# Attention units taken in pairs: scores and V products of neighbouring pairs in one break of the projection stream, transposes in another, and a new layout of PSUM

## The chip, the core and the metric

The kernel runs on one core of one Trainium2 chip. The time is the device time of one execution, in microseconds, and the figure for a kernel is the median of its runs. Engines are called by their names in the profile: PE (TensorE, with PEld for its weight loads), DVE (VectorE), ACT (ScalarE), POOL (GpSimd) and SP (SyncE, which issues most of the DMAs). "L187" is line 187 of the kernel.

## What is computed

One decoder layer over 256 tokens of width 1024, in fp32. The hidden state is normalised and projected once; two attention mixers read the projections; their results are merged through gates; then a feed-forward layer and a last normalisation follow. Cut to what matters here:

```python
h = rmsnorm(x, norm1_g[layer]);  proj = h @ w_in[layer]
# mixer A ("n"): 8 heads in 2 groups; compressed, selected and window branches
y_nsa  = gate0 * softmax(q kc) vc + gate1 * softmax(q_r ks) vs + gate2 * softmax(q_r kw) vw
# mixer B ("m"): 8 heads, causal attention with their own k and v
y_moba = softmax(qm km) vm
mixed = sig(gm[:, :1024]) * (y_nsa @ w_up_nsa) + sig(gm[:, 1024:]) * (y_moba @ w_up_moba)
x = x + mixed @ w_out
x = x + relu(rmsnorm(x, norm2_g) @ w_ff1) ** 2 @ w_ff2
return rmsnorm(x, norm_f_g)
```

With 256 tokens, all four selected blocks of 64 are always taken, and the window of 512 and the block of 256 cover everything, so the selected, window and block branches are plain causal attention.

## The kernel before

**The stream of chunks.** All weights are cut into 60 chunks of up to 128 x 2048 numbers (`CHUNKS`, L20). Each chunk is loaded by one DMA into `raw`, and split into two parts for the matmuls: `whi` by ACT (L87) and `wlo` by DVE (L89, `raw - whi`). A product is then three matmuls: high by high, high by low, low by high (`mm3`). There are three buffers of each; the split for chunk c+2 is made while PE works on chunk c, in two halves. The activations (`hTh`, `hTl` and so on) are split in the same way.

**Slots and events.** The time that PE spends on one chunk is a slot. The program calls `at(pos, f, ...)` to put an event at a position from 0 to 1 of the coming slot, and `run_slot` then issues the slot's matmuls in order and calls each event when its position is reached; events of one position keep the order in which they were put. The schedule is manual: each engine gets its instructions in exactly this order and takes them in this order. The usual events of a slot are the two halves of `whi` at 0.0 and 0.45 and the two halves of `wlo` at 0.3 and 0.46 (`std_events`). A projection slot (chunks 0 to 11) has 24 matmuls of 384 to 512 columns, a slot of the merge gates (chunks 12 to 19, "gm") has 48 of 256 columns.

**Attention between the projections.** Attention is cut into 12 units (`UNITS`): for each pair of heads p of mixer A one unit with the selected keys (b = 1) and one with the window keys (b = 2), and for mixer B one unit per pair of heads. Unit u runs in slots u+8 and u+9:

- `u_scores` (0.02): scores of two heads into the PSUM tile `S`, one bank per head, as 64-row matmuls two at a time; the first 128 queries go in exact fp32, the others by three matmuls of split parts.
- `u_max` (0.03, DVE): mask, row maxima, times -0.125.
- `u_exp` (0.34, ACT): four exponentials with row sums into `P`.
- `u_norm` (0.38, DVE): sums to factors, with the branch's gate for mixer A, and `P` times factor.
- `u_trans` (0.25 of the next slot): three transposes per head on PE into two `tp` banks; ACT copies one to `PT`, DVE the other.
- `u_pv` (0.8): products with V as 64-column matmuls into the bank `yb`; ahead of them, once per p of mixer A, the compressed branch (`bdv` by `pcT`, 30 rows). `u_yevac` (0.9): split into `yTh` (ACT) and `yTl` (DVE).

Around these stand, in the same slots, the rotary embedding (`rope`, DVE) and the transposes of the heads (`transp_heads`) of the next section, the compressed branch's probabilities (`cmp_scores`, `cmp_probs_t`), the evacuation of each section (`evac_tm`, ACT), and in the gm slots `gm_evac` of the slot before (0.5: DVE multiplication L568, then ACT tanh L570).

**PSUM.** Eight banks: three `acc` in turn, one `yb`, two `tp`, two for `S`. In the feed-forward stage `tp` and `S` give way to four banks `o`.

Of the kernel before, what the change touches and what calls it, by code (L numbers as in the profile page):

```python
# [8 lines left out]
F32 = mybir.dt.float32  # L9
F32R = mybir.dt.float32r  # L10
AF = mybir.ActivationFunctionType
ALU = mybir.AluOpType
# [28 lines left out]
def hybrid_layer(ctx: ExitStack, tc: tile.TileContext, gxd, w, w1c, small, const, gf, out):  # L41
# [6 lines left out]
    ps_acc = ctx.enter_context(tc.tile_pool(name="ps_acc", bufs=3, space=PS))  # L48
    ps_y = ctx.enter_context(tc.tile_pool(name="ps_y", bufs=1, space=PS))
    at_stack = ExitStack()  # L50
    ap_ = at_stack.enter_context(tc.tile_pool(name="att", bufs=1))
    ps_t = at_stack.enter_context(tc.tile_pool(name="ps_t", bufs=2, space=PS))
    ps_s = at_stack.enter_context(tc.tile_pool(name="ps_s", bufs=1, space=PS))
    ctx.enter_context(tc.manual_schedule())

    def acc_tile():
        return ps_acc.tile([128, 512], F32, name="acc")

    def tp_tile():
        return ps_t.tile([128, 512], F32, name="tp")  # L60
# [39 lines left out]
    warm = ps_y.tile([128, 512], F32, name="yb")  # L100
# [4 lines left out]
    kc_ = cp.tile([128, K_N], F32, name="kc")  # L105
    w1 = ap_.tile([128, 2, 16, 64], F32, name="w1", tag="w1")
# [192 lines left out]
    bdv = ap_.tile([128, 128], F32, name="bdv")  # L299
# [4 lines left out]

    def cmp_gather(s):
        tp = ps_y.tile([128, 512], F32, name="yb") if s else ps_s.tile([128, 2, 512], F32,
                                                                       name="S")[:, 0]
# [48 lines left out]
    pcT = ap_.tile([32, 4, 256], F32, name="pcT")  # L356
# [38 lines left out]
    UNITS = [("n", p, b) for p in range(4) for b in (1, 2)] + [("m", p, 0) for p in range(4)]  # L395

    def u_scores(u):
        kind, p, b = UNITS[u]
        qs = qrT if kind == "n" else qmT
        kk, kp = (ksT if b == 1 else kwT, 0) if kind == "n" else (kmT, p)  # L400
        S = ps_s.tile([128, 2, 512], F32, name="S")
# [504 lines left out]
```

## Time and profile before

| | us |
|---|---|
| median of 3 runs | 395.99 |
| lowest, highest | 395.7, 398.17 |
| the profiled execution's own time | 396.34 |
| its span, first to last instruction | 394.5 |
| PE busy in the span | 384.6 (97%) |
| DVE busy | 267.5 (68%) |
| ACT busy | 204.6 (52%) |
| POOL busy | 9.0 (2%) |
| from 59 to 163 us, the slots with attention units: PE, DVE, ACT busy of 104.0 | 104.0, 86.8, 62.0 |
| mean granted clock of PE | 0.99 |

The profile is of one execution. A timeline gives for each instruction, or run of like ones, its start and its length in microseconds, the engine, the line, the operation, the output and inputs with their shapes, and in brackets how long the engine stood idle before it and whose work ended that. Neighbouring instructions of one engine overlap, so the distance between two starts says what an instruction costs the queue. The ends of matmuls are modelled. A table of windows gives busy time of PE, PEld, DVE, ACT and POOL in a stretch, with counts, then the granted clock of PE as a share of full speed, and the DMA engines' share and rate.

### The profile page before, as it was taken

How to read it: one execution, taken by the hardware profiler on the slowest of the kernel's cores; microseconds unless marked ns; L12 is line 12 of the kernel's file. 1: busy time of each engine (PE TensorE's matmuls, PEld its weight loads, DVE VectorE, ACT ScalarE, POOL GpSimd, SP SyncE). 2: the span in 40 equal slices, each digit the busy share in tenths (PEclk: the TensorE clock that was granted, in tenths of full speed). 3: DMA queues.
4: the chain of work that ended last, by engine and by line, in shares of the span. 5: the costliest groups of instructions: out<-in, count | busy, mean ns of one | idle time of the engine just before them, and what ended most of it. 6: DMA issues, size and time to landing. Idle time of an engine off the chain costs nothing.

```text
span 394.5 us, 6611 instructions
## 1 busy us (share of the span) xinstructions
PE 384.6 (97%) x2687; PEld 346.3 (88%) x2687; DVE 267.5 (68%) x468; ACT 204.6 (52%) x366; POOL 9.0 (2%) x16
## 2 busy tenths in 40 slices
PE   7999999999999999999999999999999999999993
PEld 5888887778988999999999999999998888888883
DVE  5988589798778788867866665666566443444444
ACT  6474546667645555644464556455655563334412
POOL 4300000000000000000000000000000000000001
PEclk8799999999999999999999999999999999999999
DMA  7885623523323343263482655455544637555003
GB/s 240 313 339 214 213 106 114 207 89 126 108 108 107 124 157 149 108 214 106 171 311 96 226 214 185 154 197 213 185 154 195 213 130 268 169 184 208 1 2 106
DMA packets 11694, 66.34 MB, mean 168 GB/s; under 512 B 1296, under 2 KB 3600, under 8 KB 4368
## 3 DMA queue, kind: packets, MB, share of 16 engines
q1 hardware_dynamic: 11232, 65.14, 45.8%
q10 hardware_dynamic: 432, 0.79, 0.5%
q8 instruction: 21, 0.34, 0.3%
q14 instruction: 9, 0.07, 0.1%
HBM read 64.87 MB, written 1.05 MB: 167 GB/s over the span
## 4 chain that ended last, share of the span: by engine, by line
PE 93%; issue 2%; DMA 1%; DVE 1%; ACT 1%; SPq 0%; POOL 0%; POOLq 0%; DVEq 0%
PE acc L187 62%; PE o L187 21%; PE yb L187 3%; PE S L187 2%; PE tp L450 2%; PE tp L187 1%; DMA gx<-in_gx_dram 1%; PE tp L263 1%; DVE wlo L89 0%; PE acc L719 0%; POOL rstd L164 0%; PE tp L387 0%; SPq L71 0%; SPq L114 0%; DVE x L772 0%
## 5 line engine op out<-in xcount | busy, mean ns | idle before, releaser
L89 DVE TENSOR_TENSOR wlo<-raw,whi 128x1024 fp32r<-128x1024 f32 (+2 forms) x128 | 144.4, 1159 | 41.6 <-ACT whi L87 41.5
L87 ACT ACTIVATE whi<-raw 128x1024 fp32r<-128x1024 f32 (+2 forms) x128 | 124.1, 990 | 92.2 <-issue 35.5
L187 PE MATMUL acc<-h2h,whi 128*128 128x256 f32 x256 | 71.9, 281 | 0.0
L187 PE MATMUL acc<-h2l,whi 128*128 128x256 f32 x256 | 71.9, 281 | 0.0
L187 PE MATMUL acc<-h2h,wlo 128*128 128x256 f32 x256 | 71.9, 281 | 0.0
L187 PE MATMUL o<-whi,sqh 128*128 128x512 f32 (+1 forms) x128 | 49.5, 386 | 0.0
L187 PE MATMUL o<-whi,sql 128*128 128x512 f32 (+1 forms) x128 | 49.4, 386 | 0.0
L187 PE MATMUL o<-wlo,sqh 128*128 128x512 f32 (+1 forms) x128 | 49.4, 386 | 0.0
L187 PEld LDWEIGHTS acc<-h2h,whi 128*128 128x128 f32 x256 | 49.2, 192 | 0.0
L187 PEld LDWEIGHTS acc<-h2l,whi 128*128 128x128 f32 x256 | 48.0, 188 | 0.0
L187 PEld LDWEIGHTS acc<-h2h,wlo 128*128 128x128 f32 x256 | 48.0, 188 | 0.0
L187 PE MATMUL acc<-wlo,hTh 128*128 128x512 f32 (+2 forms) x96 | 38.7, 403 | 2.0 <-DVE wlo L89 1.8
L187 PE MATMUL acc<-whi,hTh 128*128 128x512 f32 (+2 forms) x96 | 38.1, 397 | 0.1
L187 PE MATMUL acc<-whi,hTl 128*128 128x512 f32 (+2 forms) x96 | 37.8, 394 | 0.0
L187 PE MATMUL acc<-hTh,whi 128*128 128x256 f32 x128 | 37.6, 293 | 0.0
L187 PE MATMUL acc<-hTl,whi 128*128 128x256 f32 x128 | 36.9, 289 | 0.0
L187 PE MATMUL acc<-hTh,wlo 128*128 128x256 f32 x128 | 36.2, 282 | 0.0
L187 PEld LDWEIGHTS o<-wlo,sqh 128*128 128x128 f32 x128 | 24.0, 188 | 4.9
L187 PEld LDWEIGHTS o<-whi,sql 128*128 128x128 f32 x128 | 24.0, 188 | 4.9
L187 PEld LDWEIGHTS o<-whi,sqh 128*128 128x128 f32 x128 | 24.0, 188 | 4.7
L187 PEld LDWEIGHTS acc<-hTh,whi 128*128 128x128 f32 x128 | 24.3, 190 | 1.4 <-issue 1.4
L187 PEld LDWEIGHTS acc<-hTl,whi 128*128 128x128 f32 x128 | 24.3, 190 | 1.0
(216 smaller groups left out, 613.5 us busy)
## 6 DMA issues: line engine op xcount, KB each, us to landing
raw<-in_ff_dram SPq DMA_DIRECT2D x32, 1024.0 KB, 4.8
raw<-in_gm_dram SPq DMA_DIRECT2D x8, 1024.0 KB, 4.8
raw<-in_wout_dram SPq DMA_DIRECT2D x4, 1024.0 KB, 4.9
raw<-in_q_dram SPq DMA_DIRECT2D x2, 1024.0 KB, 5.6
raw<-in_qm_dram SPq DMA_DIRECT2D x2, 1024.0 KB, 5.3
raw<-in_km_dram SPq DMA_DIRECT2D x2, 1024.0 KB, 4.9
raw<-in_vm_dram SPq DMA_DIRECT2D x2, 1024.0 KB, 4.8
raw<-in_upn_dram SPq DMA_DIRECT2D x2, 1024.0 KB, 4.7
```

What stands on the lines that cost most here:

```text
L87: act.activation(hi[c][:, a:b], raw[c][:, a:b], AF.Copy)
L89: dve.tensor_tensor(lo[c][:, a:b], raw[c][:, a:b], hi[c][:, a:b].bitcast(F32), op=ALU.subtract)
L187: pe.matmul(o, l, r, start=start, stop=stop, skip_group_check=True)
L263: pe.transpose(tp[:, j * 256 + t * 128:j * 256 + t * 128 + 128], src[:, t, (2 * i + j) * 128:(2 * i + j + 1) * 128], ident)
L450: pe.transpose(tp[:, dst:dst + 128], P[:, j, src:src + 128], ident)
```

## The change

Units are taken in pairs (`PAIRS`): the two branches of one p of mixer A, or two pairs of heads of mixer B. Pair d has slots 8 + 2d (even) and 9 + 2d (odd):

- even slot, 0.02: `d_scores` of pair d (four banks of `S`; the exact matmuls of both units at the end), and right behind it `d_pv` of pair d-1; 0.04 `d_yevac` of pair d-1; 0.05 `d_max`; 0.31 and 0.44 `d_exp` of the first and the second unit; 0.7 `d_norm`.
- odd slot, 0.5: `d_trans`: twelve transposes back into the banks of `S`, two copies of twice the width (ACT the first unit, DVE the second), and for mixer A the compressed branch's product, now over all 128 rows of `bdv` and `pcT`, which are zeroed at the start by POOL.

The softmax's DVE instructions work on both units at once: two masks and two row maxima of twice the width, and two multiplications of `P` by broadcast factors in place of eight by a scalar. `P` and `PT` have one buffer of twice the size in place of two.

PSUM: `S` has four banks, `acc` two (three from the second gm slot on, with `tp`), `tp` and `yb` one each. Until slot 9 `tp` and `yb` take turns for transposes. The first `S` also takes both transposes of `cmp_gather` and the accumulators of section "kvb"; the last one takes the four `o` banks of the second feed-forward product. The transposes of heads in slots 9 and 11 go from 0.5 and 0.65 to 0.3 and 0.75.

Of the diff, the core (lines that go away with `u_max` to `unit_events` are in the listing above and left out here):

```diff
...
+    ps = ctx.enter_context(tc.tile_pool(name="ps", bufs=1, space=PS))
...
+    turn = {"acc": ["acc0", "acc1"], "tp": ["tp", "yb"]}
+    def next_bank(kind):
+        t = turn[kind]
+        t.append(t.pop(0))
+        return bank(t[-1], kind)
     def acc_tile():
-        return ps_acc.tile([128, 512], F32, name="acc")
+        return next_bank("acc")
     def tp_tile():
-        return ps_t.tile([128, 512], F32, name="tp")
+        return next_bank("tp")
+    def s_tile():
+        return ps.tile([128, 4, 512], F32, name="S", tag="S")
...
+    pcT = ap_.tile([128, 4, 256], F32, name="pcT")
+    bdv = ap_.tile([128, 128], F32, name="bdv")
+    pool.memset(pcT, 0.0)
+    pool.memset(bdv, 0.0)
...
+    PAIRS = [[("n", p, 1), ("n", p, 2)] for p in range(4)] + [
+        [("m", p, 0), ("m", p + 1, 0)] for p in (0, 2)]
+    def d_scores(d):
+        S = s_tile()
         rows = [slice(j * 64, (j + 1) * 64) for j in range(2)]
-        for x, (a, b_) in enumerate(((1, 1), (1, 2), (2, 1))):
-            for j, r in enumerate(rows):
-                mm(S[:, j, 128:384], qs[a][r, p, :], kk[b_][r, kp, :], x == 0, x == 2)
-        for j, r in enumerate(rows):
-            mm(S[:, j, 0:128], qs[0][r, p, :], kk[0][r, kp, :], True, True)
-        d = {"S": S, "P": ap_.tile([128, 2, 384], F32, name="P", bufs=2),
-             "st": ap_.tile([128, 4, 4], F32, name="ust", bufs=2)}
-        U[u] = d
-
-    def u_max(u):
-        S, st = U[u]["S"], U[u]["st"]
-        for j in range(2):
-            v = S[:, j, :].rearrange("p (a b) -> p a b", a=4)[:, 0:3:2, :]
-            dve.tensor_tensor(v, v, cmask[:, None, :].to_broadcast([128, 2, 128]), op=ALU.add)
-        dve.tensor_reduce(st[:, 0, 0:2], S[:, :, 0:128], op=ALU.max, axis=AX)
-        dve.tensor_reduce(st[:, 0, 2:4], S[:, :, 128:384], op=ALU.max, axis=AX)
+        late = []
+        for x, (kind, p, b) in enumerate(PAIRS[d]):
+            qs = qrT if kind == "n" else qmT
+            kk, kp = (ksT if b == 1 else kwT, 0) if kind == "n" else (kmT, p)
+            for i, (a, b_) in enumerate(((1, 1), (1, 2), (2, 1))):
+                for j, r in enumerate(rows):
+                    mm(S[:, 2 * x + j, 128:384], qs[a][r, p, :], kk[b_][r, kp, :], i == 0, i == 2)
+            late += [(S[:, 2 * x + j, 0:128], qs[0][r, p, :], kk[0][r, kp, :])
+                     for j, r in enumerate(rows)]
+        for o, l, r in late:
+            mm(o, l, r, True, True)
+        U[d] = {"S": S, "P": ap_.tile([128, 4, 384], F32, name="P"),
+                "st": ap_.tile([128, 4, 8], F32, name="ust", bufs=2)}
+    def d_max(d):
+        S, st = U[d]["S"], U[d]["st"]
+        v = S.rearrange("p x (a b) -> p x a b", a=4)[:, :, 0:3:2, :]
+        for x in range(2):
+            w = v[:, 2 * x:2 * x + 2]
+            dve.tensor_tensor(w, w, cmask[:, None, None, :].to_broadcast([128, 2, 2, 128]),
+                              op=ALU.add)
+        dve.tensor_reduce(st[:, 0, 0:4], S[:, :, 0:128], op=ALU.max, axis=AX)
+        dve.tensor_reduce(st[:, 0, 4:8], S[:, :, 128:384], op=ALU.max, axis=AX)
         dve.tensor_scalar(st[:, 1], st[:, 0], -0.125, None, op0=ALU.mult)
+    def d_exp(d, x):
+        S, st, P = U[d]["S"], U[d]["st"], U[d]["P"]
         for t, a, b in ((0, 0, 128), (1, 128, 384)):
+            for j in (2 * x, 2 * x + 1):
+                i = t * 4 + j
                 act.activation(P[:, j, a:b], S[:, j, a:b], AF.Exp, scale=0.125,
                                bias=st[:, 1, i:i + 1], accum_out=st[:, 2, i:i + 1])
+    def d_norm(d):
+        st, P = U[d]["st"], U[d]["P"]
         dve.tensor_scalar(st[:, 2], st[:, 2], 1.0e-30, None, op0=ALU.max)
         dve.reciprocal(st[:, 3], st[:, 2])
+        kind, p, _ = PAIRS[d][0]
         if kind == "n":
+            v = st[:, 3].rearrange("p (t x h) -> p x t h", t=2, x=2)
+            for x in range(2):
+                dve.tensor_tensor(v[:, x], v[:, x], gates[:, 1 + x, p], op=ALU.mult)
+        for t, a, c in ((0, 0, 128), (1, 128, 384)):
+            v = P[:, :, a:c]
+            dve.tensor_tensor(v, v, st[:, 3, 4 * t:4 * t + 4, None].to_broadcast([128, 4, c - a]),
                               op=ALU.mult)
+    def d_trans(d):
+        S, P = U[d]["S"], U[d]["P"]
+        kind, p, _ = PAIRS[d][0]
+        PT = ap_.tile([128, 4, 384], F32, name="PT")
+        U[d]["PT"] = PT
+        for x in range(2):
+            for j in (2 * x, 2 * x + 1):
+                for c in (0, 128, 256):
+                    pe.transpose(S[:, j, c:c + 128], P[:, j, c:c + 128], ident)
+            v = slice(2 * x, 2 * x + 2)
+            if x == 0:
+                act.activation(PT[:, v], S[:, v, 0:384], AF.Copy)
             else:
+                dve.tensor_copy(PT[:, v], S[:, v, 0:384])
+        if d == 0:
+            U["y"] = bank("yb", "yb").rearrange("p (a q) -> p a q", a=2)
+        if kind == "n":
+            mm(U["y"][:, p % 2], bdv, pcT[:, p, :], True, False)
+    def d_pv(d):
+        PT = U[d]["PT"]
+        for x, (kind, p, b) in enumerate(PAIRS[d]):
+            y = U["y"][:, p % 2]
+            for t, n0 in ((0, 0), (1, 128)):
+                for j in range(2):
+                    if kind == "n":
+                        v = kvb[:, t, b * 128 + j * 64:b * 128 + (j + 1) * 64]
+                    else:
+                        v = vm[:, t, (2 * p + j) * 64:(2 * p + j + 1) * 64]
+                    rhs = PT[:, 2 * x + j, 0:256] if t == 0 else PT[:, 2 * x + j, 256:384]
+                    mm(y[j * 64:(j + 1) * 64, n0:256], v, rhs, kind == "m" and t == 0,
+                       t == 1 and (kind == "m" or b == 2))
+    def d_yevac(d):
+        kind, p, _ = PAIRS[d][0]
+        n = 1 if kind == "n" else 2
+        y = U["y"][:, p % 2:p % 2 + n]
+        h, l = yTh[kind][:, p:p + n, :], yTl[kind][:, p:p + n, :]
+        act.activation(h, y, AF.Copy)
+        dve.tensor_tensor(l, y, h.bitcast(F32), op=ALU.subtract)
+    def unit_events(s):
+        d, odd = (s - 8) // 2, s % 2
+        if not 8 <= s <= 20:
             return
+        if odd:
+            at(0.5, d_trans, d)
+            return
+        if d < 6:
+            at(0.02, d_scores, d)
+        if d > 0:
+            at(0.02, d_pv, d - 1)
+            at(0.04, d_yevac, d - 1)
+        if d < 6:
+            at(0.05, d_max, d)
+            at(0.31, d_exp, d, 0)
+            at(0.44, d_exp, d, 1)
+            at(0.7, d_norm, d)
...
-        accs = [acc_tile(), acc_tile()]
+        accs = [S_first[:, 2], S_first[:, 3]] if sec == "kvb" else [acc_tile(), acc_tile()]
...
-                at(0.5, transp_heads, tm["qm"], qmT, 0)
-                at(0.65, transp_heads, tm["qm"], qmT, 1)
+                turn["tp"] = ["tp"]
+                at(0.3, transp_heads, tm["qm"], qmT, 0)
+                at(0.75, transp_heads, tm["qm"], qmT, 1)
...
-                at(0.5, transp_heads, tm["km"], kmT, 0, False)
-                at(0.65, transp_heads, tm["km"], kmT, 1, False)
+                at(0.3, transp_heads, tm["km"], kmT, 0, False)
+                at(0.75, transp_heads, tm["km"], kmT, 1, False)
...
+        if i == 1:
+            turn["acc"].append("tp")
...
-    ops = {p: FB["o"].tile([128, 512], F32, name=f"o{p[0]}_{p[1]}") for p in PARTS[0] + PARTS[1]}
+    So = s_tile()
+    ops = {p: So[:, i] for i, p in enumerate(PARTS[0] + PARTS[1])}
...
```

More of the change, by code (lines that the diff above doesn't have):

```diff
@@ L713, in x1_rows @@
     def x1_rows():
-        tiles = [acc_tile(), acc_tile(), acc_tile(), ps_y.tile([128, 512], F32, name="yb")]
+        tiles = [acc_tile(), acc_tile(), acc_tile(), bank("yb", "yb")]
         for k2 in range(4):
@@ L812, in hybrid_layer @@
         else:
-            ops[LAST[1]] = ps_y.tile([128, 512], F32, name="yb")
+            ops[LAST[1]] = bank("yb", "yb")
             at(0.05, first_part)
```

80 lines of the change are left out of this document (5 added, 75 removed).

## The prediction

> **What bounds the kernel now.** I read the page first: span, and the chain of work that ended last.
>
> ```profile
> span 394.5 us, 6611 instructions
> ```
>
> ```profile
> PE 93%; issue 2%; DMA 1%; DVE 1%; ACT 1%; SPq 0%; POOL 0%; POOLq 0%; DVEq 0%
> ```
>
> The chain that sets the end is TensorE's own instruction stream for 93% of the span. So a change in the attention stage has two prices: what it does to the length of that stream, and any wait that it puts into it. For both I read the timeline of that stage, engine by engine. First TensorE around one unit's scores (columns: start, duration, engine, line, operation, tiles, count):
>
> ```profile
> 102.27 0.28 PE L187 MATMUL acc<-hTh,wlo 128*128 128x256 f32 x1
> 102.39 0.28 PE L187 MATMUL acc<-hTh,whi 128*128 128x256 f32 x1
> 102.60 0.39 PE L187 MATMUL S<-kwh,qrh 64*128 64x256 f32 x2
> 102.82 0.28 PE L187 MATMUL S<-kwl,qrh 64*128 64x256 f32 x2
> 102.94 0.28 PE L187 MATMUL S<-kwh,qrl 64*128 64x256 f32 x2
> 103.06 0.39 PE L187 MATMUL S<-kw,qr 64*128 64x128 f32 x4
> 103.37 0.38 PE L187 MATMUL acc<-hTl,whi 128*128 128x256 f32 x1
> 103.59 0.28 PE L187 MATMUL acc<-hTh,wlo 128*128 128x256 f32 x1
> ```
>
> Starts tell more than durations, because neighbours overlap. The projection's matmuls start 0.12 us apart (102.27, 102.39). Around the change to 64-row matmuls the steps are 0.21 or 0.22 instead (102.39 to 102.60, 102.60 to 102.82, 103.37 to 103.59), about 0.1 more each time. From 102.39 to 103.59 are 1.20 us where two steps of the stream would take 0.24: this break costs 0.96. Then a transposition, and the V products with the compressed branch ahead of them:
>
> ```profile
> 104.79 0.82 PE L450 MATMUL tp<-ident,P 128*128 128x128 f32 x6
> 105.36 0.36 PE L187 MATMUL acc<-hTh,whi 128*128 128x256 f32 x1
> 105.56 0.28 PE L187 MATMUL acc<-hTl,whi 128*128 128x256 f32 x1
> ...
> 108.55 0.28 PE L187 MATMUL acc<-hTh,wlo 128*128 128x256 f32 x1
> 108.76 0.69 PE L187 MATMUL yb<-pcT,bdv 30*128 30x256 f32 x2
> 109.38 0.87 PE L187 MATMUL yb<-PT,kvb 128*64 128x256 f32 x8
> 110.18 0.39 PE L187 MATMUL acc<-hTh,whi 128*128 128x256 f32 x1
> 110.40 0.28 PE L187 MATMUL acc<-hTl,whi 128*128 128x256 f32 x1
> ```
>
> Six transposes take 0.57 and 0.08 of delay behind them (0.20 for 0.12): 0.65. The V products cost 0.21 + 0.80 + 0.22 - 0.24 = 0.99, the compressed branch before them 0.62 (108.76 to 109.38).
>
> **Part 1, TensorE's stream.** A pair of units costs now 2 x 0.96 + 2 x 0.99 + 2 x 0.65 = 5.20, and 5.82 with the compressed branch (the four "n" pairs). Afterwards:
> - The joint break has 0.98 (102.39 to 103.37) for one unit's scores, 0.57 for the other's (three more steps of 0.12, and 0.21 for the second pair of exact matmuls: the 0.31 from 103.06 to 103.37 without 0.1 for the change of shape), 0.70 and 0.80 for two units' V products (the first saves the 0.1 of leaving), 0.22, less 0.24: 3.03.
> - The transposing break has 12 transposes: 0.65 + 0.57 = 1.22, and in "n" pairs the compressed branch, now over all 128 rows: 0.62 less the two changes of shape, 0.42.
>
> So 4.67 instead of 5.82 in four pairs and 4.25 instead of 5.20 in two: 6.5 us less. Pair 0's scores and pair 5's V products stand in breaks of their own, which gives back about 0.3. **TensorE gains 6.2 us.** Bounds: if the change from 64 rows to 64 columns inside the break costs more than 0.1 or the zeroed rows help less, 4; if the second unit slots in closer, 8.
>
> **Part 2, the wait behind it.** What used to be two loads of softmax work in two slots is now one load in the even slot, and its result P must be there when TensorE reaches the transposes, at position 0.5 of the odd slot. One unit of before on VectorE (DVE), with the work that stands between:
>
> ```profile
> 112.47 0.90 DVE L416 TENSOR_TENSOR S<-S,kc 128x256 f32<-128x256 f32 x2 [1.60 <-PE S L187]
> 113.40 0.42 DVE L417 TENSOR_REDUCE ust<-S 128x2 f32<-128x256 f32 x1
> 113.74 0.68 DVE L418 TENSOR_REDUCE ust<-S 128x2 f32<-128x512 f32 x1
> ...
> 116.48 0.17 DVE L432 TENSOR_SCALAR ust<-ust 128x4 f32<-128x4 f32 x1 [0.18 <-ACT P L426]
> ...
> 117.10 1.01 DVE L440 TENSOR_SCALAR P<-P,ust 128x128 f32<-128x128 f32 x4
> 118.02 1.22 DVE L89 TENSOR_TENSOR wlo<-raw,whi 128x1024 fp32r<-128x1024 f32 x1
> 119.16 0.68 DVE L568 TENSOR_TENSOR sga<-acc,rb 128x512 f32<-128x512 f32 x1
> 120.81 0.42 DVE L481 TENSOR_TENSOR yTln<-yb,yThn 128x256 fp32r<-128x256 f32 x1 [0.97 <-ACT yThn L480]
> ```
>
> and on ScalarE (ACT), from the first of four exponentials to the split behind them:
>
> ```profile
> 114.73 0.36 ACT L426 ACTIVATE P<-S,ust 128x128 f32<-128x128 f32 x1
> ...
> 116.33 1.07 ACT L87 ACTIVATE whi<-raw 128x1024 fp32r<-128x1024 f32 x1
> ...
> 120.41 0.37 ACT L480 ACTIVATE yThn<-yb 128x256 fp32r<-128x256 f32 x1
> ```
>
> The engines take their work in the order of the source's events, as these rows stand: now the normalisation (event 0.38) is ahead of the second wlo (0.46) and of the gate multiplication L568 (0.5). In the new order d_norm is at 0.7, behind both. And the second wlo needs the second whi (event 0.45), which ACT now has behind all eight exponentials (0.31 and 0.44). I add up a pair whose even slot is a gate slot, from that slot's first matmul:
> - The V products end, and the stream resumes, at 0.98 + 0.57 + 0.70 + 0.80 = 3.05; ACT starts yTh about 0.1 later, 3.16. DVE's yTl follows 0.40 later (120.41 to 120.81) and takes some 0.34 on the queue: 3.90. d_max is queued behind it, so the maxima now wait for the V products too.
> - Elements cost DVE 0.26 us per 256 (0.42 and 0.68 of the reductions). Two masks of 512: 2 x (0.47 + 0.26) = 1.46; the reduction of 512: 0.60 (0.34 for 256, 113.40 to 113.74, and 0.26); from the start of the other one to the first exponential 1.51 (0.99 for 512, 113.74 to 114.73, and 0.52): 7.47.
> - Eight exponentials: 2 x 1.60 = 3.20 (114.73 to 116.33): 10.67. whi 1.07, DVE can start the wlo at 11.8, 1.14 (118.02 to 119.16): 12.95. L568: 13.6.
> - Normalisation: four small instructions at 0.21 (116.48 to 117.10 has three): 14.45; products of 512 (0.60) and of 1024 (1.14): **P is ready at 16.2.**
> - TensorE: even slot 48 x 0.12 + 3.03 = 8.79, half the odd slot 2.88: it is there **at 11.67**. It can begin on the columns of the first product, about 0.1 of work, then waits: 4.4.
>
> Queued behind the waiting transposes on TensorE is everything: the rest of the odd slot and the next pair's scores, with which the next chain begins. So the wait doesn't wear off; it comes back with each pair. DVE's own backlog adds nothing: after 16.2 it has two wlo, the PT copy (some 0.9) and L568, until about 20.1; TensorE starts the next pair near 16.2 + 1.2 + 0.4 + 2.9 = 20.7.
>
> The other pairs: gate pair 2 has no L568 yet (less 0.68), rb's evacuation among its exponentials, and its transposes put TensorE about 0.3 later: 3.7. Pairs 4 and 5 lack the two gate multiplications (less 0.4): 4.0; pair 5 has a yTh of twice the width before its maxima (two times 0.26): 4.5. Pairs 0 and 1 stand in projection slots, with a rope in L568's place:
>
> ```profile
> 80.85 0.28 DVE L253 TENSOR_TENSOR ropa<-qtm,kc 128x128 f32<-128x128 f32 x1
> ```
>
> ```profile
> 63.97 1.05 ACT L389 ACTIVATE pcT<-tp 30x512 f32<-30x512 f32 x2
> ```
>
> The rope's eight instructions (at most 8 x 0.28) stand ahead of the wlo that waits over 3 us for ACT, and are covered. A projection slot has 24 matmuls of 512 columns; I take twice the gate slot's step, 0.24. Pair 1: P 0.68 earlier without L568 and 0.12 later by the longer first matmul, 15.6; TensorE has one more transposition of heads before it (four transposes, 0.45 by the six above), 12.1: 3.4. Pair 0 has no V products and no yTl ahead of its maxima, which start at 0.24 + 0.98 + 0.57 = 1.8, and pcT's 1.05 among the exponentials: P at 14.4. TensorE: 5.76 + 1.53 for the scores alone + 0.85 for eight transposes of the compressed branch + 0.45 + 2.88 = 11.5: 2.8. **Sum of the waits: 2.8 + 3.4 + 3.7 + 4.4 + 4.0 + 4.5 = 22.8 us.** Bounds: if a wide DVE instruction cost only what a narrow one does, the chain loses about 2.3 and the sum is near 10; if each cost two narrow ones, it gains 1 and the sum is near 30.
>
> **Part 3, edits at nothing.** Memory set to zero on POOL for pcT and bdv:
>
> ```profile
> 4.18 1.04 POOL L152 TENSOR_TENSOR xsq<-gx 128x512 f32<-128x512 f32 x1 [2.79 <-DMA gx<-in_gx_dram]
> ```
>
> The 2.79 us in which POOL waits for x cover a fill of 1024 columns even at two such rows, 2.1; uncovered it would delay only xsq. Two acc banks in the projections: the second is read at the end of its group, and written again a half slot later. One tp bank for the heads: the first's evacuation has 0.45 of a slot, 2.6 us. The ff stages get as many banks as they had.
>
> **Sum.** The profiled execution took 396.34 (394.5 span and 1.8 around it), 0.35 above the median of 395.99: 396.3 - 6.2 + 22.8 = **413 us**.
>
> **Rivals.**
> 1. The clock falls in the waits. The trace has one such place, at the start:
>
> ```profile
> 5.69 0.44 PE L187 MATMUL acc<-wlo,hTh 128*128 128x384 f32 x1 [0.98 <-DVE wlo L89]
> ```
>
> ```profile
> 5.50:7.20 1.70, 1.46 (x6) 1.01 (x6) 0.85 (x3) 0.69 (x2) 0.12 (x1) 1.00 1.00 326
> 9.00:11.00 2.00, 1.37 (x4) 0.86 (x4) 2.00 (x2) 2.00 (x6) 2.00 (x2) 0.50 1.04 386
> ```
>
> TensorE idled for about a microsecond, and some 2 us later the granted clock (third column from the end) was 0.50. Waits of 2.8 to 4.5 might do the same each time. Between the transposes and the next V products lie some 7.5 us of path; a stretch of 3.5 to 7 us at half clock there adds 1.7 to 3.5, six times: 423 to 434. Against it: the start is the only case, with other causes possible. Chance 0.20. The Trainium skill ("TensorE: Matmul & The Clock Gate", section "Why this matters for your kernels") says to avoid gaps of TensorE above some 3 us, since one idle window takes the clock back to half; by that rule nearly every one of my waits is long enough, and the result would be this rival's. No wait of that length stands in this trace between matmuls.
>
> 2. Half the wait: the wide instructions are cheap, or the transposes overlap more of P than I count. Waits of 2 us: 396.3 - 6.2 + 12 = 402. For it: the lower bound of the sum. Chance 0.10.
>
> 3. Faster: P is there in time and only part 1 is left: 390. The place is the sum to 16.2; it decides below 11.7, so it must lose 4.5. Taking out whi, wlo and L568 from between (2.9) isn't enough, and the order of the source puts them there; the wide forms' 2.3 would have to come on top. Chance 0.06. Just short of it, waits of 1 us, 396: 0.03.
>
> 4. The breaks don't get cheaper, since each change of shape inside costs as it does now: 2 us of the 6.2 go, 415; within my case.
>
> **Numbers.** My forecast, with its bounds, has 0.61, rivals 1 and 2 0.20 and 0.10, the rest 0.09. A measurement of this kernel tells 1% from no change, 392 to 400: faster 0.06, same 0.03, slower 0.91. The range goes from 403, just above rival 2, to 430, half-way into rival 1's.
>
> **What would show it.** In the waits of TensorE: six waits for P by DVE's products in d_norm, 2.5 to 5 us each, ahead of the first transposes of each pair, and an odd slot's end about 20 us after its pair's start. On ACT, whi directly behind eight exponentials, and on DVE an idle stretch that ends with it. Breaks: near 3.0 and 1.6 us. Granted clock 1.0 from 59 us on if rival 1 is wrong. If TensorE doesn't wait at the transposes, the sum of part 2 is wrong, and with it the forecast.

## The result, and the profile after

| | before | after |
|---|---|---|
| median of 4 runs each, us | 396.99 | 442.31 |
| lowest, highest | 395.7, 398.17 | 441.72, 444.98 |
| the profiled execution's own time, and its span | 396.34, 394.5 | 444.98, 443.2 |

The ratio is 1.1146, with a 95% interval of 1.1087 to 1.1205: 45 us slower where 17 were forecast. The profiled execution of after is the longest of its four. Of its page, the span, the granted clock in 40 slices, and the chain that ended last:

```profile
span 443.2 us, 6505 instructions
...
PEclk9668999998897969696999999999999999999999
...
PE 75%; DVE 11%; ACT 8%; issue 4%; DMA 1%; SPq 1%; POOL 0%; POOLq 0%; DVEq 0%; ACTq 0%
```

TensorE's own stream was 93% of the chain and is now 75%; DVE has 11%, ACT 8%. And there are sixes in the clock row in the slices of the attention slots. Cut at the first matmul of each stage, the two traces differ so (worked out from starts, idle times and the record of the granted clock; idle is TensorE's):

| stage | before: us, idle, at half clock | after: us, idle, at half clock | difference |
|---|---|---|---|
| up to section kvb | 19.19, 3.17, 6.83 | 20.87, 4.89, 6.83 | +1.7 |
| section kvb | 13.13, 0.44, 0 | 22.69, 6.31, 10.24 | +9.6 |
| section q | 26.91, 0, 0 | 26.91, 0, 0 | 0 |
| slots 8 to 19, with attention units | 102.80, 0, 0 | 140.75, 27.13, 37.55 | +38.0 |
| up-projections, w_out | 46.75, 0, 0 | 45.18, 0, 0 | -1.6 |
| first feed-forward product | 90.45, 0, 0 | 87.04, 0, 0 | -3.4 |
| second feed-forward product | 89.16, 0, 0 | 93.45, 3.21, 0 | +4.3 |

Behind the last of these stages 0.1 us more is left, of 48.6 in the spans.

The largest waits of TensorE after (columns: who waits for whom, us in total, times, longest):

```profile
PE S L474 <- DVE P L462: 18.7, 11, 3.5
PE S L474 <- ACT PT L477: 5.7, 6, 1.0
PE S L204 <- DVE kE L335: 5.2, 2, 3.6
PE acc L204 <- DVE wlo L101: 3.5, 4, 1.4
PE S L474 <- ACT whi L99: 2.7, 1, 2.7
PE S L204 <- DVE x L805: 2.5, 3, 0.8
```

L474 are the transposes: 18.7 + 5.7 + 2.7 = 27.1 us of waits, all the idle time of the attention slots. The row with ACT's whi is the first wait of pair 1, and so one for P as well: there DVE's first product of P starts at 105.85, and the transposes at 106.69. The timeline of TensorE around pair 2, the first whose even slot is a gate slot:

```profile
116.29 0.28 PE L204 MATMUL acc<-hTh,whi 128*128 128x256 f32 x1
116.50 0.38 PE L204 MATMUL S<-ksh,qrh 64*128 64x256 f32 x2
...
117.86 1.52 PE L204 MATMUL yb<-PT,kvb 128*64 128x256 f32 x16
119.31 0.39 PE L204 MATMUL acc<-hTl,whi 128*128 128x256 f32 x1
119.53 0.28 PE L204 MATMUL acc<-hTh,wlo 128*128 128x256 f32 x1
...
131.04 0.37 PE L474 MATMUL S<-ident,P 128*128 128x128 f32 x1 [2.76 <-DVE P L462]
132.09 1.33 PE L474 MATMUL S<-ident,P 128*128 128x128 f32 x5 [0.67 <-DVE P L462]
134.37 1.54 PE L474 MATMUL S<-ident,P 128*128 128x128 f32 x6 [0.96 <-ACT PT L477]
```

The joint break takes 119.53 - 116.29 = 3.24, less two steps of 0.12: 3.00 us. The transposes wait three times: for the first product of P, for the second, and, half-way through, for ACT's copy of the first unit. On DVE, in the same pair:

```profile
120.19 1.42 DVE L437 TENSOR_TENSOR S<-S,kc 128x512 f32<-128x512 f32 x2
...
128.35 1.23 DVE L101 TENSOR_TENSOR wlo<-raw,whi 128x1024 fp32r<-128x1024 f32 x1 [3.56 <-ACT whi L99]
...
130.20 1.83 DVE L462 TENSOR_TENSOR P<-P,ust 128x512 f32<-128x512 f32 x2
131.94 2.35 DVE L101 TENSOR_TENSOR wlo<-raw,whi 128x1024 fp32r<-128x1024 f32 x2
```

DVE stands idle for 3.56 us behind ACT's whi, then makes the wlo, and only then normalises; the next instruction can start at 131.94, so P is ready some 15.7 us after the slot's start. The windows of the attention slots, in the kernel before (first line) and after, and of three stretches of this pair (columns as explained above; the granted clock is third from the end):

```profile
59.23:162.03 102.80, 102.80 (x788) 88.05 (x788) 86.18 (x210) 61.32 (x159) 0.00 (x0) 1.00 0.35 124
70.47:211.22 140.75, 113.62 (x786) 99.09 (x786) 79.49 (x126) 61.60 (x154) 0.00 (x0) 0.87 0.28 98
116.29:119.53 3.24, 3.24 (x39) 2.45 (x38) 0.40 (x1) 1.74 (x3) 0.00 (x0) 1.00 0.01 3
119.53:131.04 11.51, 8.75 (x73) 8.57 (x73) 7.44 (x14) 6.72 (x21) 0.00 (x0) 1.00 0.04 11
131.04:137.80 6.76, 5.12 (x20) 4.29 (x21) 4.82 (x5) 1.00 (x2) 0.00 (x0) 0.51 0.70 257
```

As TensorE resumes, the clock is at half for the next 6.8 us. And in section kvb, again on TensorE:

```profile
22.57 0.27 PE L327 MATMUL S<-ident,kcd 128*128 128x128 f32 x1
23.29 0.55 PE L327 MATMUL S<-ident,kcd 128*128 128x128 f32 x3 [0.45 <-ACT kcd L257]
27.45 0.71 PE L204 MATMUL S<-whi,hTl 128*128 128x408 f32 x1 [3.62 <-DVE kE L335]
...
32.27 0.71 PE L204 MATMUL S<-whi,hTl 128*128 128x408 f32 x1 [1.55 <-DVE kE L335]
```

The projection (L204) accumulates into banks 2 and 3 of the first `S`; the two groups of transposes of `cmp_gather` (L327) write banks 0 and 1. After each group the projection stands still until DVE has read the gathered banks into kE (L335), though it doesn't touch them.

### The profile page after: what moved, and what is told of

Read it like the earlier page. It is cut to its first block, busy times and chain, and to the rows that moved or that the text cites. A ratio compares the mean times of both kernels' runs of the same rounds, so it can differ in the third digit from the quotient of the medians.

```text
span 443.2 us, 6505 instructions
## 1 busy us (share of the span) xinstructions
PE 395.4 (89%) x2687; PEld 355.2 (80%) x2687; DVE 260.4 (59%) x382; ACT 204.8 (46%) x358; POOL 10.1 (2%) x18
## 4 chain that ended last, share of the span: by engine, by line
PE 75%; DVE 11%; ACT 8%; issue 4%; DMA 1%; SPq 1%; POOL 0%; POOLq 0%; DVEq 0%; ACTq 0%
PE acc L204 43%; PE S L204 23%; ACT P L448 4%; PE S L474 4%; PE yb L204 3%; DVE wlo L101 2%; DVE P L462 2%; DVE S L437 1%; ACT whi L99 1%; DVE ust L440 1%; DMA gx<-in_gx_dram 1%; ACT PT L477 1%; PE tp L204 1%; DVE ust L439 1%; DVE kE L335 1%
## 5 line engine op out<-in xcount | busy, mean ns | idle before, releaser
L204 PE MATMUL acc<-h2h,whi 128*128 128x256 f32 x256 | 70.7, 276 | 0.0
L204 PE MATMUL acc<-h2l,whi 128*128 128x256 f32 x256 | 70.7, 276 | 0.0
L204 PE MATMUL acc<-h2h,wlo 128*128 128x256 f32 x256 | 70.7, 276 | 0.0
L204 PE MATMUL S<-whi,sql 128*128 128x512 f32 (+1 forms) x128 | 49.6, 388 | 1.7 <-DVE x L805 1.7
L204 PE MATMUL S<-whi,sqh 128*128 128x512 f32 (+1 forms) x128 | 49.6, 388 | 1.5 <-DVE x L805 0.8
L204 PE MATMUL S<-wlo,sqh 128*128 128x512 f32 (+1 forms) x128 | 49.4, 386 | 0.0
L204 PEld LDWEIGHTS acc<-h2h,whi 128*128 128x128 f32 x256 | 48.1, 188 | 0.0
L204 PEld LDWEIGHTS acc<-h2l,whi 128*128 128x128 f32 x256 | 48.1, 188 | 0.0
L204 PEld LDWEIGHTS acc<-h2h,wlo 128*128 128x128 f32 x256 | 48.1, 188 | 0.0
L474 PE MATMUL S<-ident,P 128*128 128x128 f32 x72 | 18.2, 403 | 27.1 <-DVE P L462 18.7
L204 PE MATMUL acc<-hTh,whi 128*128 128x256 f32 x128 | 38.8, 303 | 0.0
L474 PEld LDWEIGHTS S<-ident,P 128*128 128x128 f32 x72 | 12.4, 202 | 32.3 <-ACT whi L99 8.5
L204 PE MATMUL acc<-hTl,whi 128*128 128x256 f32 x128 | 38.0, 297 | 0.0
L204 PE MATMUL acc<-hTh,wlo 128*128 128x256 f32 x128 | 37.5, 293 | 0.0
L204 PE MATMUL acc<-wlo,hTh 128*128 128x512 f32 (+1 forms) x80 | 33.3, 416 | 3.5 <-DVE wlo L101 3.5
L204 PE MATMUL acc<-whi,hTh 128*128 128x512 f32 (+1 forms) x80 | 34.1, 426 | 0.0
L204 PE MATMUL acc<-whi,hTl 128*128 128x512 f32 (+1 forms) x80 | 32.5, 406 | 0.0
L448 ACT ACTIVATE P<-S,ust 128x128 f32<-128x128 f32 (+1 forms) x48 | 19.5, 428 | 23.6 <-DVE ust L441 23.6
L204 PEld LDWEIGHTS S<-whi,sql 128*128 128x128 f32 x128 | 24.0, 188 | 7.3 <-DVE x L805 2.5
L204 PEld LDWEIGHTS S<-whi,sqh 128*128 128x128 f32 x128 | 24.0, 188 | 6.8 <-issue 1.1
```

What stands on the lines that cost most here:

```text
L204: pe.matmul(o, l, r, start=start, stop=stop, skip_group_check=True)
L448: act.activation(P[:, j, a:b], S[:, j, a:b], AF.Exp, scale=0.125, bias=st[:, 1, i:i + 1], accum_out=st[:, 2, i:i + 1])
L474: pe.transpose(S[:, j, c:c + 128], P[:, j, c:c + 128], ident)
```

## The experiments

My theory was: (a) P is late, as forecast; (b) the clock falls behind these waits and costs more than 10 us; (c) the four banks of `S` are one tile, and a matmul that writes one of them is held until the reads of the others are done. Rivals: a slower stream or a backlog of DVE, half clock without a price, and, for (c), accumulation or transposes that are slow by themselves.

**The gather into banks of its own.**

```diff
-        tp = S_first[:, s]
+        tp = tp_tile()
```

> The changed kernel, with the two transposes of cmp_gather in banks of their own (tp and yb in turn) instead of in the first two banks of S. Theory (a tile of four banks counts as one: matmuls into banks 2 and 3 of the first S wait for VectorE's reads of banks 0 and 1): the waits for kE (5.2 us in all) go, the clock stays at 1.0 after 25 us, and the kvb section takes 13 us instead of 22.7, so the time falls by 9 to 10 us, to about 433. Rival (the transposes themselves, or the missing third acc bank, hold TensorE there): the section stays above 20 us and the time at 442.

Measured: 436.37 us (434.67 and 438.06), span 432.9. Section kvb takes 14.18 us in place of 22.69 and has no stretch at half clock; the attention slots are as they were (140.8). So the wait was that of the tile, not of the section's work, and of its 9.6 us this gives back 8.5; the rest of the span's 10.3 is in the stage before it (19.17 in place of 20.87). By the medians the gain is 5.9 us, less than the 9 to 10 expected, from two runs that lie 3.4 us apart.

**All twelve transposes ahead of both copies.**

```diff
-            v = slice(2 * x, 2 * x + 2)
-            if x == 0:
-                act.activation(PT[:, v], S[:, v, 0:384], AF.Copy)
-            else:
-                dve.tensor_copy(PT[:, v], S[:, v, 0:384])
+        act.activation(PT[:, 0:2], S[:, 0:2, 0:384], AF.Copy)
+        dve.tensor_copy(PT[:, 2:4], S[:, 2:4, 0:384])
```

> The changed kernel, with all twelve transposes of a pair issued ahead of the two copies out of S, instead of six, copy, six, copy. Theory (the second six wait for ScalarE's copy of the first unit, although it reads other banks): the six waits for the PT copy (5.7 us in all) go, and the time falls by 6 to 9 us, to about 434. Rival (the copies come later now, and the next scores, which need S free, or the V products wait instead): as much idle time of TensorE as before, ahead of the scores, and 442.

Measured: 433.55 us (431.62 and 435.47), span 433.7. No wait for PT at the transposes is left, while the waits for P stand as before; the attention slots take 131.3 in place of 140.8, of which 5.7 are these waits; the rest goes with the clock, which is at half there for 27.3 us in place of 37.6. The wait half-way through the transposes was again that of the one tile: the second unit's transposes write other banks than those that ACT reads.

**The normalisation ahead of the second wlo and of the gate multiplication.**

```diff
-            at(0.7, d_norm, d)
+            at(0.455, d_norm, d)
```

> The changed kernel, with d_norm at 0.455 instead of 0.7 of the even slot: ahead of the second wlo and of the gate multiplication on VectorE. Theory (P comes late since it is queued behind these two): P comes 1.1 us earlier in pairs 0 to 2 and 1.8 us in pairs 3 to 5, 9 us in all, so at most 433; if the waits that are left, about 1.6 us, no longer take the clock down, 15 us less again, about 418. Rival (the exponentials and maxima alone are too long, or wlo comes late for the stream instead): 440 or more, with new waits for wlo.

Measured: 432.51 us (431.61 and 433.41), span 429.8. Two waits of TensorE:

```profile
PE S L474 <- ACT PT L477: 15.5, 6, 4.2
PE S L474 <- DVE P L462: 7.5, 11, 0.8
```

The waits for P fall from 21.4 (18.7 + 2.7) to 7.5, as the order says, but the wait for PT grows from 5.7 to 15.5: three of its six are 4.22 us. ACT between two transposings shows why:

```profile
141.33 0.63 ACT L601 ACTIVATE sga<-sga 128x512 f32<-128x512 f32 x1 [3.40 <-DVE sga L599]
141.87 1.99 ACT L99 ACTIVATE whi<-raw 128x1024 fp32r<-128x1024 f32 x2
143.76 0.79 ACT L477 ACTIVATE PT<-S 128x768 f32<-128x768 f32 x1
```

TensorE has P earlier, but the copy that releases the second half of its transposes stands on ACT behind a tanh (L601) that waits for DVE, and behind two whi. Of 27.1 us of waits 23.0 are left, at another place: P's lateness can't be judged by this edit without that of the copies.

**Both edits, and yT behind the maxima.** The copies and the normalisation as above, and

```diff
-            at(0.04, d_yevac, d - 1)
+            at(0.06, d_yevac, d - 1)
```

> e2_copies, with two events moved: d_norm to 0.455 as in e3_norm, and d_yevac from 0.04 to 0.06, behind d_max, so that the masks and maxima no longer wait for the V products on VectorE. Theory (only the length of the softmax chain in the queues makes P late): P is ready some 11 us after the even slot's first matmul, when TensorE comes to the transposes; waits for P under 0.5 us a pair, granted clock 1.0 from the first scores on, the stage from the first scores to the last gate slot about 97 us instead of 141, the time near 400. Rival (another queue takes over, such as ScalarE's copy behind the tanh, or the V products): a new wait of 1 us or more a pair, the clock falls again, above 410.

Measured: 403.34 us (402.91 and 403.78), ratio to the kernel before 1.0161 (1.0109 to 1.0214). The attention slots:

```profile
68.35:169.13 100.78, 97.24 (x786) 88.13 (x786) 76.80 (x124) 60.26 (x153) 0.00 (x0) 1.00 0.34 125
```

The same 786 matmuls as in after (113.62 busy us) take 97.24, and 3.5 us of idle time are left of 27.1. The granted clock is 1.00. What the change lost in these slots came from the order of the copies and two events, with no instruction less. What each of the two events gives by itself, with the copies in order, was not measured.

**Matmuls in place of the wait.** The question was what the clock costs. On top of the edit of the copies, 26 products that TensorE doesn't need are put ahead of the transposes; they go into the half of `yb` that the next product overwrites, so only time is added.

```diff
+        if d == 0:
+            U["y"] = bank("yb", "yb").rearrange("p (a q) -> p a q", a=2)
+        for _ in range(26):
+            mm(U["y"][:, p % 2], hTh[:, 0, 0:128], hTh[:, 0, :], True, True)
         for x in range(2):
```

> What e4_fill was for, without its new waits: e2_copies, with 26 matmuls of 256 columns (about 3.1 us, results unused) on TensorE ahead of the transposes of each pair, into the part of bank yb that is written next, acc as in e2_copies. They add work that nobody needs, into time in which TensorE waits for P. Theory (the idle wait takes the clock down, and that costs 2 to 3 us a pair): granted clock 1.0 from the first scores on, the stage from there to the last gate slot some 12 us shorter than in e2_copies, about 422. Rival (the clock falls for another reason, or costs nothing): clock low in five or six places and 433 or more.

Measured: 423.49 us (423.2 and 423.77). The extra products of one pair, and the transposes behind them:

```profile
119.86 3.28 PE L204 MATMUL yb<-hTh 128*128 128x256 f32 x26
122.98 0.27 PE L478 MATMUL S<-ident,P 128*128 128x128 f32 x1
123.82 1.42 PE L478 MATMUL S<-ident,P 128*128 128x128 f32 x11 [0.57 <-DVE P L462]
```

and the windows of the attention slots, first of the kernel with the copies' edit alone, then of this one:

```profile
70.46:201.76 131.30, 109.91 (x786) 98.09 (x786) 79.38 (x126) 61.38 (x154) 0.00 (x0) 0.90 0.28 103
```

```profile
68.60:189.49 120.89, 117.00 (x942) 106.93 (x942) 79.25 (x126) 61.03 (x154) 0.00 (x0) 1.00 0.30 106
```

With 6 x 26 = 156 useless matmuls more the slots are 10.4 us shorter, because the clock stays at 1.00: P is no earlier (in pair 2 of both kernels 15.65 us after the pair's start), TensorE just doesn't stand idle for it. A start every 0.12 us (122.98 - 119.86 for 26) makes 18.7 for 156; without them 117.00 - 18.7 = 98.3 us of busy time stand against 109.91 at the falling clock. So the half clock cost that kernel 11.6 us, and it does so by slowing the matmuls between the transposes and the next scores, which lie on the path.

A first form of this run put 24 such products into a `tp` bank, with two `acc` banks through the gate slots:

> e2_copies, with 24 matmuls of 256 columns (about 2.9 us, into the tp bank, results unused) on TensorE ahead of the transposes of each pair, where it waits for P; acc has two banks through all gate slots for that. They add work that nobody needs. Theory (the idle wait takes the clock down to 0.50 for one or two stretches of 3.4 us, and that costs 2 to 3 us a pair): granted clock 1.0 through the attention slots, and about 15 us less than e2_copies, near 420. Rival (the clock falls for another reason, or its fall costs nothing because TensorE waits anyway): the clock stays low in six places and the time is that of e2_copies or some us more.

It took 453.18 us (452.38 and 453.97) and says nothing on the clock: taking `tp` away made new waits (15.0 us of TensorE for an acc bank, 10.0 for tp), and the clock fell in those.

**All repairs together.** The order and the gather as above, and `S` in a pool of the attention stage, so that the last product gets four tiles of one bank each.

```diff
+    ps_s = at_stack.enter_context(tc.tile_pool(name="ps_s", bufs=1, space=PS))
...
-        return ps.tile([128, 4, 512], F32, name="S", tag="S")
+        return ps_s.tile([128, 4, 512], F32, name="S", tag="S")
...
-    So = s_tile()
-    ops = {p: So[:, i] for i, p in enumerate(PARTS[0] + PARTS[1])}
+    ops = {p: FB["o"].tile([128, 512], F32, name=f"o{p[0]}_{p[1]}") for p in PARTS[0] + PARTS[1]}
```

> e5_order with cmp_gather's banks as in e1_gather, and with S in a pool of its own, so that the last product has four tiles of one bank instead of one of four. Theory (the loss is the late P, the clock behind it, and the waits of tiles that count as one): no wait of TensorE over 0.5 us after the first section, attention breaks as cheap as forecast (6 us less than before), the last product as before, so about 389, faster than the kernel before. If the gate and feed-forward stages keep the pace of the changed kernel (feed-forward 87.0 instead of 90.5 us), about 385. Rival (the new layout costs something else, or the breaks give nothing): 396 or more.

Measured: 396.32 us (392.0 to 400.93, 10 runs), ratio 0.9958 (0.9926 to 0.999), where the theory had 389 or less. The second feed-forward product takes 89.13 us in place of 93.45, without a wait. Section kvb still takes 19.47, with one wait on TensorE:

```profile
28.18 0.34 PE L205 MATMUL S<-whi,hTl 128*128 128x408 f32 x1
31.92 0.45 PE L205 MATMUL S<-whi,hTh 128*128 128x408 f32 x1 [3.39 <-ACT kvb L261]
```

and on ACT

```profile
29.38 2.00 ACT L100 ACTIVATE whi<-raw 128x1024 fp32r<-128x1024 f32 x2 [3.22 <-DMA raw<-in_q_dram]
```

The second accumulator of kvb waits until ACT has read the first: the neighbouring bank of the same tile once more, in the one place that these repairs left. ACT reads it at 31.29, behind two whi that wait for the DMA of section q's chunk; in the trace of the gather's edit alone, where this idle time of ACT is 0.63 instead of 3.22, the same wait of TensorE is 0.81.

**kvb into two tiles of one bank each**, closed before the first `S` is opened:

```diff
-        accs = [S_first[:, 2], S_first[:, 3]] if sec == "kvb" else [acc_tile(), acc_tile()]
+        accs = ([ps_k.tile([128, 512], F32, name=n_) for n_ in ("k0", "k1")] if sec == "kvb"
+                else [acc_tile(), acc_tile()])
```

> The three repairs of e7_all (gather into a bank of its own, order of the softmax's work, last product in tiles of its own), and section kvb accumulates into two tiles of one bank each, which give way to S before the first scores. Theory (the rest of the kvb section's loss is the same wait as in the gather: a matmul into one bank held until ACT has read the neighbouring bank of the same tile): the one wait of 3.4 us for ACT's evacuation of kvb is gone, with it the half clock behind it; section kvb takes 13.1 to 13.3 us in place of e7_all's 19.47, q 26.91 in place of 27.30, the rest as in e7_all, span 389 to 390, time 390 to 391, 1.5% below the kernel before. Rival (the evacuation itself is late, whatever the tiles): the wait stays near 3.4 us and the time near 396.

Measured: 390.27 us (390.05 to 395.05, 5 runs), ratio 0.9857 (0.9834 to 0.988). Section kvb takes 13.13 us, as before the change; the wait is gone.

**The transposes a little earlier**, on top of that:

```diff
-            at(0.5, d_trans, d)
+            at(0.455, d_trans, d)
```

> e9_kvb with the transposes' event at 0.455 of the odd slot in place of 0.5, so that ACT's and DVE's copies of PT are queued ahead of the second wlo of that slot. Theory (the 2.8 us that TensorE's scores still wait in e7_all are for DVE's copy of PT, which is queued behind a wlo): these waits fall below 1 us in all and the time is 1 to 3 us below e9_kvb. Rival (P isn't ready before 0.5 of the odd slot): waits for P at the transposes take their place, 0.3 to 1 us for each of six pairs, and the time is the same or up to 3 us more.

Measured: 390.06 us (389.16 to 390.95, 4 runs), ratio 0.9844 (0.9822 to 0.9866). The two waits of the scores for PT go from 2.8 to 1.7 us and not below 1, as the theory had it, and the waits for P from 0.7 to 0.9. Against the run before that is no difference that four or five runs can tell. The attention slots:

```profile
60.84:161.12 100.28, 97.45 (x786) 88.14 (x786) 76.68 (x123) 59.96 (x153) 0.00 (x0) 1.00 0.35 125
```

and in the first gate pair, which begins at 94.53, the maxima and P on DVE, and the transposes on TensorE:

```profile
96.21 1.43 DVE L440 TENSOR_TENSOR S<-S,kc 128x512 f32<-128x512 f32 x2 [1.28 <-PE S L209]
...
104.15 1.83 DVE L465 TENSOR_TENSOR P<-P,ust 128x512 f32<-128x512 f32 x2
105.90 2.35 DVE L106 TENSOR_TENSOR wlo<-raw,whi 128x1024 fp32r<-128x1024 f32 x2
```

```profile
106.12 1.47 PE L477 MATMUL S<-ident,P 128*128 128x128 f32 x12
```

P is ready 11.4 us after the pair's start, TensorE arrives after 11.6 and doesn't wait. By its median this version is about 1.5% below the kernel before. The attention slots are only a part of that. Stage by stage its trace is 2.5 us below before's in these slots, 4.6 below in the three stages behind them, where no edit explains the gain (see the end), and 1.6 above ahead of them. The profiled execution of the version with kvb in two tiles has no such gain behind the slots, and took 395.05 us where that of the kernel before took 396.34.

**The bank numbers, and the rows of the compressed branch.** Two runs looked for the cause of a gain that no part of the change explains: the first feed-forward product, with the same instructions, takes 87.04 us in place of 90.45. One is the kernel before with its PSUM banks in another order (`yb` in bank 0, `tp` in 1 and 2, `S` in 3 and 4, `acc` in 5 to 7; the last product in the banks of `tp` and `S`), done by opening the pools in that order. The other is the kernel before with this edit of the change alone:

```diff
-    pcT = ap_.tile([32, 4, 256], F32, name="pcT")
+    pcT = ap_.tile([128, 4, 256], F32, name="pcT")
+    pool.memset(pcT, 0.0)
+    pool.memset(bdv, 0.0)
...
-            mm(y, bdv[0:30, :], pcT[0:30, p, :], True, False)
+            mm(y, bdv, pcT[:, p, :], True, False)
```

> The kernel before, with PSUM laid out anew and nothing else of the change: yb in bank 0, tp in 1 and 2, S in 3 and 4, the three acc in 5 to 7 (before: acc in 0 to 2, yb in 3, tp in 4 and 5, S in 6 and 7); the last product takes the tp banks and the two of S. Theory (the first feed-forward product went from 90.5 to 87.0 us in the changed kernel because of the banks that its accumulators have): 87.0 here too, the sections up and wout 0.7 and 0.9 us less, so about 391. Rival (that gain has another cause): 90.5, and 396.

> The kernel before with one part of the change alone: pcT and bdv set to zero over all 128 rows by POOL, and the compressed branch's product over 128 rows in place of 30. Theory A (the stages after attention run faster in every paired kernel, ff1 87.04 in place of 90.45 us, because no matmul of 30 rows precedes them): ff1 near 87.0, up 23.4, w_out 21.8, time about 391. Theory B (it has another cause): ff1 stays 90.45, and only the four products get cheaper by 0.2 us each and POOL's fill stays hidden: 395 to 396.5.

Measured: 397.28 us (ratio 1.0016, 0.9998 to 1.0034) and 395.81 us (0.9979, 0.996 to 0.9999), 10 runs each. In both the stage stays at 90.45. Neither alone is the cause.

## Why the prediction was wrong, step by step

The sign was right, and so was the mechanism that it put first. In the sum 396.3 - 6.2 + 22.8 the terms stand so:

- **Part 1, TensorE's stream, 6.2 us less: right, a little large.** At full clock the attention slots' matmuls take 97.45 us (the version with the transposes a little earlier) in place of 102.80: 5.35 less. The joint break took 3.00, forecast 3.03; the transposing one, in that version's pair 2, 1.74, forecast 1.64.
- **Part 2, the waits for P, 22.8 us: right.** They sum to 18.7 + 2.7 = 21.4. Pair by pair, first and second wait together, they are 2.77, 3.46, 3.43, 3.87, 3.65 and 4.22, against 2.8, 3.4, 3.7, 4.4, 4.0 and 4.5. The chain is as it was worked out: whi behind eight exponentials, DVE idle until it is done (3.56), wlo, then the normalisation; P ready after 15.7 us in pair 2, where 16.2 - 0.68 = 15.5 was forecast. Neither bound of the wide instructions was needed (the two products cost the queue 131.94 - 130.20 = 1.74 us, forecast 0.60 + 1.14).
- **Failed: the clock in the waits.** The sum of 413 has no term for it; rival 1 held it, with chance 0.20. Of the 32 us between that sum and the profiled execution it makes 16.2. The attention slots' 786 matmuls took 113.62 us instead of 97.45: 16.2 us, or 2.7 per pair, inside the 1.7 to 3.5 per pair that the rival worked out. The prediction's reason against the rival (only one place in the trace, with other causes possible) was no reason to put the term at nothing: the row behind the 0.98 us wait was already one of half clock. In pair 2 the half clock begins as a wait of 2.76 us ends. The Trainium skill ("TensorE: Matmul & The Clock Gate", section "Why this matters for your kernels") has the clock fall to half behind gaps above some 3 us; the traces agree in kind, and the waits that did it are shorter.
- **Failed: part 3, "Edits at nothing".** "The ff stages get as many banks as they had" is true of banks, but the wait goes by tile. I counted banks, and gave the four banks of `S` no price. They have one in three places, 19.6 us in all: 9.6 us in section kvb (6.3 of idle time, where before had 0.4, and the half clock behind it), 5.7 in the transposes, 4.3 in the last product. The prediction doesn't mention the first two at all. The other edits of part 3 cost nothing that the traces show: TensorE never waits for a bank of `acc` or `tp` in after.
- **Not foreseen: 5.0 us of gain** in the up-projections, w_out and the first feed-forward product (1.6 + 3.4), see the end.

With what was measured, the sum is 396.3 - 5.4 (stream) + 27.1 (waits at the transposes) + 16.2 (clock) + 9.6 (kvb) + 4.3 (last product) + 1.7 (start) + 0.1 (end) - 5.0 = 444.9; the profiled execution took 444.98. The 1.7 of the start is no term of the change: that stage took between 18.5 and 20.9 us in the traces of these kernels.

Rival 3, faster at 390, was right about its condition: P had to be there before 11.7, and taking out whi, wlo and L568 (2.9 us) isn't enough. What it lacked was that the maxima don't have to stand behind the V products' yT: moved ahead, they start 1.7 us after the pair's start (96.21 - 94.53) instead of 3.9 (120.19 - 116.29 in after), and P is ready at 11.4. In that order the time is the 390 that the rival named, but the number is luck in part: with 2.8 us of waits left the slots give 2.5 us of the rival's 6.2, and the rest comes from the faster stages behind them.

## What to carry to other kernels

When work is packed into fewer, larger breaks of a stream, follow the queue of each engine up to the point where the stream needs the result, and move the events (here two, with the order of two copies) until the result is there first; what the break saves is small beside one missed wait. Price a wait of the tensor engine twice: its length, and the matmuls at half clock behind it. And a tile of several banks costs waits between users of different banks: give each user of a bank that lives at the same time a tile of its own.

## What was not expected of the hardware

**Half clock comes in multiples of 3.41 us.** All stretches at half clock between the start and the end of the program last 3.41, 6.83 or 10.24 us by the clock record. The Trainium skill ("TensorE: Matmul & The Clock Gate", section "Part 1: The HAM clock gate") has the clock set by windows of about 3.4 us, and these traces agree. The length of a single wait doesn't decide alone. In the kernel with the normalisation moved, three short waits follow each other in pair 1:

```profile
97.97 0.30 PE L474 MATMUL S<-ident,P 128*128 128x128 f32 x1 [0.63 <-DVE P L462]
99.02 0.77 PE L474 MATMUL S<-ident,P 128*128 128x128 f32 x5 [0.74 <-DVE P L462]
100.75 1.54 PE L474 MATMUL S<-ident,P 128*128 128x128 f32 x6 [0.96 <-ACT PT L477]
```

In pair 2 of the same kernel there are three such waits again, of 0.69, 0.74 and 0.96. Below are windows of 3.41 us, counted from the clock's fall at 100.77 in that trace: the last one ahead of the fall and the first behind it, then the two in which the waits of pair 2 lie, and the one behind these:

```profile
97.36:100.77 3.41, 1.09 (x7) 0.69 (x7) 3.41 (x4) 3.41 (x6) 0.00 (x0) 1.00 0.00 0
100.77:104.18 3.41, 3.41 (x11) 2.98 (x12) 3.06 (x4) 0.50 (x1) 0.00 (x0) 0.50 0.85 322
117.84:121.25 3.41, 1.94 (x14) 1.34 (x12) 3.30 (x7) 2.81 (x3) 0.00 (x0) 1.00 0.00 0
121.25:124.66 3.41, 2.49 (x20) 2.44 (x21) 3.41 (x5) 0.81 (x1) 0.00 (x0) 1.00 0.57 195
124.66:128.07 3.41, 3.41 (x40) 3.08 (x40) 0.60 (x2) 1.69 (x2) 0.00 (x0) 1.00 1.00 416
```

All three waits of pair 1 lie in one window, in which TensorE is idle for 2.32 us, and behind it the clock is at half. The waits of pair 2 sum to as much, but are spread over two windows, with 1.47 and 0.92 us of idle time, and the clock stays. The 13 traces of this case, each cut at its own clock record's steps of 3.41 us, fit: behind all 33 windows at full clock with over 1.95 us of idle time the clock is at half, behind 979 of 981 with under 1.69 us it is not (the two others stand in the first 12 us of a trace), and the seven between go both ways. So it's the idle time within one such window that goes with the fall. This is read from the traces; no run moved a wait from one window to another.

**The stream of 256-column matmuls has two paces at full clock.** The groups of the first feed-forward product in the profiled executions of the last two versions (columns: busy time, mean ns of one, idle before):

```profile
L209 PE MATMUL acc<-h2h,whi 128*128 128x256 f32 x256 | 71.9, 281 | 0.0
```

```profile
L209 PE MATMUL acc<-h2h,whi 128*128 128x256 f32 x256 | 70.7, 276 | 0.0
```

The first is the version with kvb in two tiles, the second the one with the transposes moved on top of that. The starts are 0.118 us apart in the one, 0.113 in the other, from the up-projections to the end of this stage (90.45 and 87.04 us); in the gate slots before them both have 0.120. The first version's profiled execution took 395.05 us with a span of 393.3; three of its other four have spans of 388.3 to 388.5. The 5 us between are about what the slow pace costs in these stages, so one program seems to show both paces. The program has a part in it all the same: the kernel before and its two variants above showed the slow pace in their profiles, none of their runs beside these experiments was below 394.9, and with the fast pace they would take about 391 (an estimate, 396.3 less the 5.0 of the stages). What sets the pace stays open: bank numbers and the 30-row product were tried and neither is it alone. So it stays open, too, how much of the 1.5% belongs to the change.
